# Attention scores as products of 64 rows, two maps in the two halves of the array

## The chip, the cores and the metric

The kernel runs on one core of a Trainium2 chip. A core has a matrix engine (TensorE, "PE" in the profile, with its weight loads listed apart as "PEld"), a vector engine (VectorE, "DVE"), a scalar engine (ScalarE, "ACT"), GpSimd ("POOL") and a sync engine ("SP") that issues most transfers. The metric is the device time of one execution in microseconds; the figure is the median of the runs.

## The reference

The program is a two-layer encoder over 1024 tokens of width 1024, all in float32. Each layer is a token mixer, a layer norm, a gated feed-forward net and another layer norm. Layer 0 mixes by latent attention, layer 1 by *differential* attention, and only that second mixer is touched here:

```python
q, k, v = split(x @ w_in)          # q, k: 8 heads x 2 maps x 64; v: 8 heads x 128
logits = einsum('bqhmd,bkhmd->bmhqk', q_b, k) * scale      # m = 2 maps, d = 64
logits = logits - slopes[:, None, None] * dist
logits = where(chunk_mask, logits, -1e30)
p = softmax(logits, axis=-1)
a = p[:, 0] - lam * p[:, 1]
o = einsum('bhqk,bkhe->bqhe', a, v)
```

So each head has two score maps. Each map contracts over only 64 numbers, which is half of the 128 rows of the matrix array. The mask lets a block of 128 queries see the keys up to its own block, so block i (0 to 7) has n = 128 (i+1) keys.

## The kernel before, in words

Precision is held by splitting every float32 operand into a high part (rounded to fp32r, a format that the array takes in one pass) and a low part (the rest). A product is then the sum of three: high by high, high by low, low by high. The helper `mm3` (lines 139 to 145) writes these three out for ordinary products: projections of queries and keys ("bp" tiles, 24 matmuls of 128x512 each), values ("bv" tiles, 24 of 128x256).

The second attention is built by `attention` (one loop over 64 blocks: 8 heads by 8 query blocks). For each block it makes the scores two blocks ahead (`score_b`), transposes the finished probabilities of this block (`turn_b`), every second block multiplies by the values (`mix_b`), and in between it runs the projections of the next head and the values of the next pair of heads out of a table of slots (`fill`). The calls give the program order. A list scheduler then interleaves the instructions of each engine by priority; scores and transposes carry a higher priority (`tc.high_priority`) than the projections, so that TensorE gets projections where the others are not ready. Each engine runs its own stream in that fixed order.

The scores need the two maps of 64 rows kept apart. Before, `proj_b` laid the data out so that *two* products of the full 128 rows make one map's scores:

- keys: one tile per map, with the high part in one half of the rows and the low part in the other half (lines 1413 and 1414, per map);
- queries, high: the high part in one half of the rows (line 1403), copied by a DMA from the POOL queue to the other half (line 1407), so that one product gives high by high plus high by low;
- queries, low: the low part in the half that faces the keys' high part (line 1404) and zeros in the other half. The zeros are written once (lines 1360 to 1366).

`softmax_block` (line 206) then does one map at a time. For each stretch of at most 512 keys (one for n up to 512, two equal ones above) it takes a bank of the accumulator memory PSUM, runs the two matmuls of line 220 (stationary: 128 queries; moving: the keys), and lets VectorE add the distance bias and take the row minimum (line 223). ScalarE takes the exponential over all n keys (line 228). Then `score_b` normalizes, GpSimd scales the second map (line 1430) and VectorE adds both (line 1431).

PSUM has eight banks in this stage. `PS_BUFS_B = (3, 2, 2, 1)` gives three to the scores (and to the sums of the head norm, "ms"), two to projections and values, two to transposes, and one to the value products. A tile of a kind takes the banks of its kind in turn.

Of the kernel before, what the change touches and what calls it, by code (L numbers as in the profile page):

```python
# [9 lines left out]
F32 = mybir.dt.float32  # L10
F32R = mybir.dt.float32r
AF = mybir.ActivationFunctionType
ALU = mybir.AluOpType
# [3 lines left out]
P = 128  # L17
S = 1024
# [16 lines left out]
BIGF = 3.0e38  # L35
PS_BUFS = (4, 2, 2)
PS_BUFS_A = (2, 3, 3)
PS_BUFS_B = (3, 2, 2, 1)
LAST_ORDER = (6, 7, 4, 5, 2, 3, 0, 1)


# [1 line left out]
def trunk(  # L43
# [32 lines left out]
    nc = tc.nc  # L76
    V, A, G, T = nc.vector, nc.scalar, nc.gpsimd, nc.tensor
# [11 lines left out]
    ps, ps_bufs, ps_stack = None, None, None  # L89
# [17 lines left out]
    def f32(t):  # L107
        return t.bitcast(F32)

    def big_tile(name, dt=F32R):  # L110
        return big.tile([P, 2, 1024], dt, tag="big", name=name)

    def ps_s(name):
        return ps.tile([P, 512], F32, tag="s", bufs=ps_bufs[0], name=name)
# [2 lines left out]
        return ps.tile([P, 512], F32, tag="m", bufs=ps_bufs[1], name=name)  # L117

    def ps_t(name):
        return ps.tile([P, 512], F32, tag="t", bufs=ps_bufs[2], name=name)  # L120

    def ps_o(name):
# [2 lines left out]
    def small(name, n=1):  # L125
        return sp.tile([P, 2], F32, tag="small", name=name, bufs=22)[:, :n]
# [28 lines left out]
    def behind(i, j):  # L155

        tc.add_manual_dep(
            i, j.name,
            mybir.DependencyInfo(mybir.DependencyClass.NoSync, mybir.DependencyReason.DATA),
            reason="kept in program order",  # L160
        )
# [48 lines left out]
    def softmax_block(lp, q_pass, s_bias, i, scale, name, sm=None):  # L210
        n = (i + 1) * P
        nb = 1 if n <= 512 else 2
        w = n // nb
        l = lp.tile([P, 1024], F32, tag="l", name=f"l_{name}")
        mx = BIGF
        for b in range(nb):
            s = ps_s(f"s_{name}_{b}")
            ks = slice(b * w, (b + 1) * w)
            for j, (lh, rh) in enumerate(q_pass):
                T.matmul(s[:, :w], lh, rh[:, ks], start=(j == 0), stop=(j == len(q_pass) - 1))  # L220
            bv = s_bias[:, 896 - P * i + b * w:896 - P * i + (b + 1) * w]
            m = small(f"mx_{name}_{b}")
            V.tensor_tensor_reduce(l[:, ks], s[:, :w], bv, -scale, mx, ALU.add, ALU.min, m)  # L223
            mx = m
        whole = sm is None
        if whole:
            sm = small(f"sm_{name}")
        ends["exp"] = A.activation(l[:, :n], l[:, :n], AF.Exp, bias=mx, scale=-1.0, accum_out=sm).ins  # L228
        if not whole:
            return l  # L230
        r = small(f"r_{name}")
        V.reciprocal(r, sm)
        return l, r
# [830 lines left out]
    with tc.tile_pool(name="a0", bufs=2, side="right") as pool:  # L1064
# [42 lines left out]
        with tc.issue_after(third):  # L1107
            kt = pool.tile([P, NTB, P], F32, tag="kt", name="kt", bufs=1)
# [83 lines left out]
    with ast as st:  # L1192
        pool = st.enter_context(tc.tile_pool(name="a1", bufs=2, reuse_waits="tile"))
        vp = st.enter_context(tc.tile_pool(name="a1v", bufs=12, side="right", reuse_waits="tile"))
        lp = st.enter_context(tc.tile_pool(name="a1l", bufs=4, side="right", reuse_waits="tile"))
# [105 lines left out]
        for h in range(1, H):  # L1301
            b = 8 * (h - 1)
# [32 lines left out]
    def split_wo(h, c):  # L1335
# [6 lines left out]
    xT, rest, normed = ffn(  # L1342
        "left", xo, stacks, pending, 0, xs_dr[0], xs_dr[1], ln_ffn_g[0], ln_ffn_b[0], next_x,
        [lambda h=h, c=c: split_wo(h, c) for h in range(H) for c in range(2)],
    )
# [3 lines left out]
    with ExitStack() as st:  # L1349
        lp = st.enter_context(tc.tile_pool(name="b1l", bufs=5, reuse_waits="tile"))  # L1350
# [2 lines left out]
        bb = pool.tile([P, S], F32, tag="bb", name="bb", bufs=1)  # L1353
        nc.sync.dma_start(bb, c_bias_b)
        vt, lt, pts, sqs, q_slot = {}, {}, {}, {}, {}
        qt = [big_tile(f"bq{j}") for j in range(2)]
        kt = [big_tile(f"bk{j}") for j in range(2)]
        ob = big_tile("bo", F32)
        q_hi = [qt[0][:, 0], qt[0][:, 1], qt[1][:, 0]]
        q_lo = [qt[1][:, 1]] + [pool.tile([P, S], F32R, tag=f"ql{j}", name=f"ql{j}", bufs=1) for j in range(2)]  # L1360
        for ql in q_lo:
            for mp in range(2):
                b = slice(64 - mp * 64, 128 - mp * 64)
                z = bb[b, :512]
                i = G.tensor_tensor(ql[b, mp * 512:mp * 512 + 512], z, z, ALU.subtract).ins
                behind(i, normed[-1][2])

        def values_b(pr, tb):
            if ("v", pr) not in wts:
# [17 lines left out]
        def proj_b(h, which, hf):  # L1387
            if (which, h) not in wts:
                wts[which, h] = load_w(w_b_qk[h, which], 1024, f"wb{h}_{which}")
            wh, wl = wts[which, h]  # L1390
            hs = slice(hf * 512, hf * 512 + 512)
            m = ps_m(f"bp{h}_{which}_{hf}")
            mm3(m, [(wh[:, k * P:k * P + P], wl[:, k * P:k * P + P], xT[0][hf][:, k, :], xT[1][hf][:, k, :])
                    for k in range(KD)])
            sc = float(2.0 ** (h + 1) / 8.0)
            if which == 0:
                j = 2 * h + (hf if h < H - 1 else 1 - hf)
                q2, ql = q_slot[h, hf] = q_hi[j % 3], q_lo[j % 3]
                for mp in range(2):
                    a = slice(mp * 64, mp * 64 + 64)  # L1400
                    b = slice(64 - mp * 64, 128 - mp * 64)
                    qh = q2[:, mp * 512:mp * 512 + 512]
                    A.activation(qh[a], m[a, :], AF.Copy, scale=sc)
                    V.scalar_tensor_tensor(
                        ql[a, mp * 512:mp * 512 + 512], m[a, :], sc, f32(qh[a]), ALU.mult, ALU.subtract
                    )
                    nc.gpsimd.dma_start(qh[b], qh[a])
            else:
                for mp in range(2):
                    a = slice(mp * 64, mp * 64 + 64)  # L1410
                    b = slice(64 - mp * 64, 128 - mp * 64)
                    k = kt[h % 2][:, mp]
                    A.copy(k[a, hs], m[a, :])
                    V.tensor_tensor(k[b, hs], m[a, :], f32(k[a, hs]), ALU.subtract)

        def score_b(h, i):
            c = slice((i % 4) * P, (i % 4) * P + P)
            n = (i + 1) * P
            (q2, ql), k = q_slot[h, i // 4], kt[h % 2]
            sm, r = small(f"smb{h}_{i}", 2), small(f"rb{h}_{i}", 2)  # L1420
            l0, l1 = [
                softmax_block(
                    lp,
                    [(t[:, m * 512:m * 512 + 512][:, c], k[:, m]) for t in (q2, ql)],
                    bb, i, float(2.0 ** -(h + 1)), f"b{h}_{i}_{m}", sm[:, m:m + 1],
                )
                for m in range(2)
            ]
            V.reciprocal(r, sm)  # L1429
            G.tensor_scalar(l1[:, :n], l1[:, :n], r[:, 1:2], nlam, ALU.mult, ALU.mult)  # L1430
            V.scalar_tensor_tensor(l0[:, :n], l0[:, :n], r[:, 0:1], l1[:, :n], ALU.mult, ALU.add)
            lt[h, i] = l0
# [67 lines left out]
        for h in range(1, H):  # L1500
            b = 8 * (h - 1)
# [124 lines left out]
```

## Time and profile before

| | |
|---|---|
| median of 3 runs | 2262.74 us (2262.04 to 2263.79) |
| the profiled execution's own time | 2264.72 us |
| its span, first to last instruction | 2263.0 us |
| TensorE busy | 2239.2 us (99%), 11410 instructions |
| VectorE, ScalarE, GpSimd busy | 1545.3, 1014.7, 776.2 us |
| mean granted TensorE clock | 0.998 |
| first and last score product of the second attention start at | 1125.8 and 1532.1 us |

The profile lists, for each engine, when each instruction ran, how long, and what the engine waited for. A matmul's record runs from its start until its result is out, so records of neighbouring matmuls overlap; how much time one takes from the stream is read from start to start. "64x512" after a name is partitions by elements. Lines are those of the kernel before.

### The profile page before, as it was taken

Reading aid. Unit: us, or ns where it says so; the run is one execution under the profiler, and the core shown is the slowest. Engines: PE = TensorE matmul, PEld = TensorE weight load, DVE = VectorE, ACT = ScalarE, POOL = GpSimd, SP = SyncE. Lnnn points to the kernel's source line nnn. Section 1 sums busy time; section 2 is a strip of 40 time slices with the busy share of each in tenths; the row PEclk is TensorE's granted clock in tenths of the full one; section 3 lists DMA queues with packets and bytes.
Section 4 is the critical chain, followed back from the end, with each engine's and each line's share of the span. In section 5 each row is a group of like instructions: output and inputs, shape, how many; then the busy total and the mean of one; then the engine's idle time right before and its main releaser. Section 6 shows DMA issues by size and latency. Waiting matters only on the chain.

```text
span 2263.0 us, 31059 instructions
## 1 busy us (share of the span) xinstructions
PE 2239.2 (99%) x11410; PEld 1912.2 (84%) x11410; DVE 1545.3 (68%) x2894; ACT 1014.7 (45%) x2097; POOL 776.2 (34%) x626
## 2 busy tenths in 40 slices
PE   8999999999999999999999999999999999999998
PEld 8999998888888888888888898878788888888886
DVE  5676765596766667777576667576787656658778
ACT  4455664352333334444465656564432333334444
POOL 2232341114444440455432424221114444430561
PEclk9999999999999999999999999999999999999999
DMA  5010125434435338454320212063344232238443
GB/s 204 14 35 31 42 71 188 147 122 155 171 133 202 115 127 327 181 194 157 99 52 22 69 34 62 23 223 124 128 144 165 82 108 102 103 113 325 162 180 150
DMA packets 105545, 287.76 MB, mean 127 GB/s; under 512 B 7968, under 2 KB 30112, under 8 KB 94896
## 3 DMA queue, kind: packets, MB, share of 16 engines
q1 hardware_dynamic: 101552, 277.44, 34.6%
q0 software_dynamic: 3840, 8.33, 1.4%
q8 instruction: 90, 1.47, 0.3%
q14 instruction: 63, 0.52, 0.1%
HBM read 204.47 MB, written 77.07 MB: 124 GB/s over the span
## 4 chain that ended last, share of the span: by engine, by line
PE 95%; DVE 2%; DMA 1%; issue 1%; ACT 1%; POOL 0%; SPq 0%; DVEq 0%; POOLq 0%; ACTq 0%
PE gb L548 15%; PE ga L548 10%; PE gc L548 10%; PE dw L872 7%; PE dx L872 5%; PE s_a L220 4%; PE zp_a L418 3%; PE s_b L220 3%; PE dv L872 3%; PE dy L872 3%; PE bp L145 3%; PE bp L143 3%; PE bp L144 3%; PE o_a L263 2%; PE o_b L263 2%; PE hq L1123 2%
## 5 line engine op out<-in xcount | busy, mean ns | idle before, releaser
L504 ACT CAST op_g<-gr 128x512 fp32r<-128x512 f32 x240 | 146.9, 621 | 377.3 <-PE gb L548 189.9
L505 POOL TENSOR_TENSOR op_g<-gr,op_g 128x512 fp32r<-128x512 f32 x104 | 146.0, 1409 | 254.1 <-ACT op_g L504 143.9
L505 DVE TENSOR_TENSOR op_h<-rh,op_h 128x512 fp32r<-128x512 f32 x152 | 142.3, 962 | 50.0 <-ACT op_h L504 50.0
L548 PE MATMUL ga<-xh_m,op_g 128*128 128x512 f32 x512 | 168.2, 389 | 0.0
L872 PE MATMUL dw<-op_w_t,op_h 128*128 128x512 f32 x660 | 151.3, 390 | 0.0
L504 ACT CAST op_h<-rh 128x512 fp32r<-128x512 f32 x152 | 91.8, 619 | 124.6 <-PE dx L872 34.9
L872 PEld LDWEIGHTS dw<-op_w_t,op_h 128*128 128x128 f32 x660 | 123.6, 188 | 25.9 <-DVE op_h L505 0.3
L228 ACT ACTIVATE l_b<-l_b,mx_b 128x256 f32<-128x256 f32 (+7 forms) x128 | 99.4, 777 | 73.2 <-DVE mx_b L223 71.2
L505 POOL TENSOR_TENSOR op_w_b<-rw_b,op_w_b 128x512 fp32r<-128x512 f32 x44 | 64.5, 1488 | 175.1 <-ACT op_w_b L504 167.8
L505 DVE TENSOR_TENSOR op_g<-gr,op_g 128x512 fp32r<-128x512 f32 x136 | 112.0, 827 | 17.4 <-ACT op_g L504 17.2
L872 PE MATMUL dx<-op_w_b,op_h 128*128 128x512 f32 x528 | 121.5, 390 | 1.0 <-DVE op_w_b L505 1.0
L1430 POOL TENSOR_SCALAR l_b<-l_b,rb,cst 128x128 f32<-128x128 f32 (+3 forms) x64 | 52.8, 825 | 198.9 <-DVE rb L1429 187.5
L872 PEld LDWEIGHTS dx<-op_w_b,op_h 128*128 128x128 f32 x528 | 98.8, 188 | 23.0 <-DVE op_w_b L505 2.6
L548 PE MATMUL gb<-t3h_f,op_g 128*128 128x512 f32 x352 | 115.5, 389 | 1.0 <-DVE tmp L637 1.0
L548 PE MATMUL gb<-t2h_f,op_g 128*128 128x512 f32 x352 | 115.4, 390 | 0.4 <-DVE op_g L505 0.4
L548 PE MATMUL gc<-t1h_f,op_g 128*128 128x512 f32 x352 | 115.6, 389 | 0.1
L548 PE MATMUL gb<-t4h_f,op_g 128*128 128x512 f32 x352 | 115.5, 389 | 0.0
L548 PE MATMUL gc<-b22h_f,op_g 128*128 128x512 f32 x352 | 115.3, 389 | 0.0
L505 POOL TENSOR_TENSOR op_g<-s,op_g 128x512 fp32r<-128x512 f32 x40 | 56.1, 1403 | 166.4 <-ACT op_g L504 158.4
L548 PEld LDWEIGHTS ga<-xh_m,op_g 128*128 128x128 f32 x512 | 96.1, 188 | 20.0
L143 PE MATMUL bp<-xT_f,h_wb 128*128 128x512 f32 x256 | 101.8, 398 | 0.0
L144 PE MATMUL bp<-xT_f,h_wb 128*128 128x512 f32 x256 | 101.5, 397 | 0.0
(388 smaller groups left out, 6690.8 us busy)
## 6 DMA issues: line engine op xcount, KB each, us to landing
gr<-in_w_gu SPq DMA_DIRECT2D x44, 1024.0 KB, 6.8
rh<-h_dr SPq DMA_DIRECT2D x28, 1024.0 KB, 4.8
h_dr<-sh SPq DMA_DIRECT2D x22, 1024.0 KB, 5.1
h_dr<-hp SPq DMA_DIRECT2D x22, 768.0 KB, 4.1
tt<-in_w_dn SPq DMA_DIRECT2D x22, 512.0 KB, 7.5
rh<-h_dr SPq DMA_DIRECT2D x12, 768.0 KB, 4.3
wo_dr<-op_pwo SPq DMA_DIRECT2D x16, 512.0 KB, 3.4
z<-xs_dr SPq DMA_DIRECT2D x16, 512.0 KB, 12.0
```

Source lines behind the costliest of these rows:

```text
L143: T.matmul(ps_out, lh, rh, start=(i == 0), stop=False)
L144: T.matmul(ps_out, lh, rl, start=False, stop=False)
L145: T.matmul(ps_out, ll, rh, start=False, stop=(i == n - 1))
L220: T.matmul(s[:, :w], lh, rh[:, ks], start=(j == 0), stop=(j == len(q_pass) - 1))
L228: ends["exp"] = A.activation(l[:, :n], l[:, :n], AF.Exp, bias=mx, scale=-1.0, accum_out=sm).ins
L263: T.matmul(po[:, c], a, b[:, j % 2, c], start=st, stop=sp_, skip_group_check=True)
L418: T.matmul(m, a[:, h, :], self.wo[h][w][:, c], start=(start and h == heads[0] and a is oh and w == 0), stop=(stop and h == heads[-1] and a ...
L504: turns["cast"] = A.copy(hi, src).ins
L505: return eng.tensor_tensor(lo, src, f32(hi), ALU.subtract).ins
L548: T.matmul(o, w[:, a, k * P:(k + 1) * P], x[b][:, k, :], start=(first and k == 0 and (a, b) == (0, 0)), stop=(k == 3 and a == 1), skip_gro ...
L872: T.matmul(o, h[:, a, c], w[:, b_], start=(first and (a, b_) == (0, 0)), stop=(last and a == 1), skip_group_check=True,).ins for a, b_ in ...
L1430: G.tensor_scalar(l1[:, :n], l1[:, :n], r[:, 1:2], nlam, ALU.mult, ALU.mult)
```

## The change

Only the scores of the second attention are written in another way. Queries and keys now keep the rows that the projection gives them: map 0 in rows 0 to 63, map 1 in rows 64 to 127, a tile for the high parts and a tile for the low parts, of queries (`q_rot`, three slots in turn) and of keys (`kt`). Their extraction from PSUM is one instruction over 128 rows on ScalarE and one on VectorE where there were two each over 64 rows. The copy by DMA and the zeroed halves go.

`score_b` no longer calls `softmax_block`. For each stretch of keys it takes two banks, one per map, and runs three pairs of matmuls: high by high, high by low, low by high, each for map 0 (rows 0 to 63) and then for map 1 (rows 64 to 127). `behind` ties each of these six matmuls after the one before it, which fixes their order among themselves; it does not keep other matmuls from standing between. The bias, minimum, exponential and all that follows are the same instructions on the same shapes.

The banks are dealt as `(5, 2, 0, 1)`: scores, norm sums and transposes take five banks in turn.

```diff
@@ -35,7 +35,7 @@
 BIGF = 3.0e38
 PS_BUFS = (4, 2, 2)
 PS_BUFS_A = (2, 3, 3)
-PS_BUFS_B = (3, 2, 2, 1)
+PS_BUFS_B = (5, 2, 0, 1)
 LAST_ORDER = (6, 7, 4, 5, 2, 3, 0, 1)
 
 
@@ -117,6 +117,8 @@
         return ps.tile([P, 512], F32, tag="m", bufs=ps_bufs[1], name=name)
 
     def ps_t(name):
+        if not ps_bufs[2]:
+            return ps_s(name)
         return ps.tile([P, 512], F32, tag="t", bufs=ps_bufs[2], name=name)
 
     def ps_o(name):
@@ -1353,17 +1355,11 @@
         bb = pool.tile([P, S], F32, tag="bb", name="bb", bufs=1)
         nc.sync.dma_start(bb, c_bias_b)
         vt, lt, pts, sqs, q_slot = {}, {}, {}, {}, {}
-        qt = [big_tile(f"bq{j}") for j in range(2)]
+        qt = big_tile("bq").rearrange("p a (b t) -> p (a b) t", b=2)
         kt = [big_tile(f"bk{j}") for j in range(2)]
         ob = big_tile("bo", F32)
-        q_hi = [qt[0][:, 0], qt[0][:, 1], qt[1][:, 0]]
-        q_lo = [qt[1][:, 1]] + [pool.tile([P, S], F32R, tag=f"ql{j}", name=f"ql{j}", bufs=1) for j in range(2)]
-        for ql in q_lo:
-            for mp in range(2):
-                b = slice(64 - mp * 64, 128 - mp * 64)
-                z = bb[b, :512]
-                i = G.tensor_tensor(ql[b, mp * 512:mp * 512 + 512], z, z, ALU.subtract).ins
-                behind(i, normed[-1][2])
+        q_more = pool.tile([P, 2, 512], F32R, tag="bq", name="bq2", bufs=1)
+        q_rot = [(t[:, j], t[:, j + 1]) for t, j in ((qt, 0), (qt, 2), (q_more, 0))]
 
         def values_b(pr, tb):
             if ("v", pr) not in wts:
@@ -1395,37 +1391,42 @@
             sc = float(2.0 ** (h + 1) / 8.0)
             if which == 0:
                 j = 2 * h + (hf if h < H - 1 else 1 - hf)
-                q2, ql = q_slot[h, hf] = q_hi[j % 3], q_lo[j % 3]
-                for mp in range(2):
-                    a = slice(mp * 64, mp * 64 + 64)
-                    b = slice(64 - mp * 64, 128 - mp * 64)
-                    qh = q2[:, mp * 512:mp * 512 + 512]
-                    A.activation(qh[a], m[a, :], AF.Copy, scale=sc)
-                    V.scalar_tensor_tensor(
-                        ql[a, mp * 512:mp * 512 + 512], m[a, :], sc, f32(qh[a]), ALU.mult, ALU.subtract
-                    )
-                    nc.gpsimd.dma_start(qh[b], qh[a])
+                qh, ql = q_slot[h, hf] = q_rot[j % 3]
+                A.activation(qh, m, AF.Copy, scale=sc)
+                V.scalar_tensor_tensor(ql, m, sc, f32(qh), ALU.mult, ALU.subtract)
             else:
-                for mp in range(2):
-                    a = slice(mp * 64, mp * 64 + 64)
-                    b = slice(64 - mp * 64, 128 - mp * 64)
-                    k = kt[h % 2][:, mp]
-                    A.copy(k[a, hs], m[a, :])
-                    V.tensor_tensor(k[b, hs], m[a, :], f32(k[a, hs]), ALU.subtract)
+                kh, kl = (kt[h % 2][:, p, hs] for p in range(2))
+                A.copy(kh, m)
+                V.tensor_tensor(kl, m, f32(kh), ALU.subtract)
 
         def score_b(h, i):
             c = slice((i % 4) * P, (i % 4) * P + P)
             n = (i + 1) * P
-            (q2, ql), k = q_slot[h, i // 4], kt[h % 2]
+            nb = 1 if n <= 512 else 2
+            w = n // nb
+            (qh, ql), (kh, kl) = q_slot[h, i // 4], (kt[h % 2][:, p] for p in range(2))
             sm, r = small(f"smb{h}_{i}", 2), small(f"rb{h}_{i}", 2)
-            l0, l1 = [
-                softmax_block(
-                    lp,
-                    [(t[:, m * 512:m * 512 + 512][:, c], k[:, m]) for t in (q2, ql)],
-                    bb, i, float(2.0 ** -(h + 1)), f"b{h}_{i}_{m}", sm[:, m:m + 1],
-                )
-                for m in range(2)
-            ]
+            l0, l1 = ls = [lp.tile([P, 1024], F32, tag="l", name=f"l_b{h}_{i}_{m}") for m in range(2)]
+            mx = [BIGF, BIGF]
+            for b in range(nb):
+                ks = slice(b * w, (b + 1) * w)
+                s = [ps_s(f"s_b{h}_{i}_{m}_{b}") for m in range(2)]
+                prev = None
+                for j, (q, k) in enumerate(((qh, kh), (qh, kl), (ql, kh))):
+                    for m in range(2):
+                        rows = slice(64 * m, 64 * m + 64)
+                        t = T.matmul(s[m][:, :w], q[rows, c], k[rows, ks], start=(j == 0), stop=(j == 2)).ins
+                        if prev is not None:
+                            behind(t, prev)
+                        prev = t
+                bv = bb[:, 896 - P * i + b * w:896 - P * i + (b + 1) * w]
+                for m in range(2):
+                    mx[m], mp = small(f"mx_b{h}_{i}_{m}_{b}"), mx[m]
+                    V.tensor_tensor_reduce(
+                        ls[m][:, ks], s[m][:, :w], bv, -float(2.0 ** -(h + 1)), mp, ALU.add, ALU.min, mx[m]
+                    )
+            for m in range(2):
+                A.activation(ls[m][:, :n], ls[m][:, :n], AF.Exp, bias=mx[m], scale=-1.0, accum_out=sm[:, m:m + 1])
             V.reciprocal(r, sm)
             G.tensor_scalar(l1[:, :n], l1[:, :n], r[:, 1:2], nlam, ALU.mult, ALU.mult)
             V.scalar_tensor_tensor(l0[:, :n], l0[:, :n], r[:, 0:1], l1[:, :n], ALU.mult, ALU.add)
```

Line numbers behind the changed places move by one or two. The three pieces below are of TensorE's stream. `s_b_5_0_0` is the score tile of block 5; before, the last two numbers are map and stretch, and so they are now. `bp` is a query or key projection, `ms` a norm sum, `pt_b` a transpose.

In the fifth head, block 5, the stream before has:

```order
L1461 MATMUL ms_0_1_13311<-sq_0_13191,ones 128x512
L143 MATMUL bp_0_1_13361<-xT_f_10052,h_wb_0_13274 128x512
L220 MATMUL s_b_5_0_0_13326<-bk_10191,bq_10189 128x384
L144 MATMUL bp_0_1_13361<-xT_f_10053,h_wb_0_13274 128x512
L220 MATMUL s_b_5_0_0_13326<-bk_10191,bq_10190 128x384
L145 MATMUL bp_0_1_13361<-xT_f_10052,l_wb_0_13275 128x512
L143 MATMUL bp_0_1_13361<-xT_f_10052,h_wb_0_13274 128x512
```

and the changed kernel at the same place:

```order
L1462 MATMUL ms_0_1_13347<-sq_0_13227,ones 128x512
L145 MATMUL bp_0_1_13401<-xT_f_10052,h_wb_0_13314 128x512
L1418 MATMUL s_b_5_0_0_13363<-bk_10190,bq 128x384
L146 MATMUL bp_0_1_13401<-xT_f_10053,h_wb_0_13314 128x512
L1418 MATMUL s_b_5_1_0_13364<-bk_10190,bq 128x384
L147 MATMUL bp_0_1_13401<-xT_f_10052,l_wb_0_13315 128x512
L1418 MATMUL s_b_5_0_0_13363<-bk_10190,bq 128x384
L145 MATMUL bp_0_1_13401<-xT_f_10052,h_wb_0_13314 128x512
L1418 MATMUL s_b_5_1_0_13364<-bk_10190,bq 128x384
L146 MATMUL bp_0_1_13401<-xT_f_10053,h_wb_0_13314 128x512
L1418 MATMUL s_b_5_0_0_13363<-bk_10190,bq 128x384
L147 MATMUL bp_0_1_13401<-xT_f_10052,l_wb_0_13315 128x512
```

The two score products of map 0 became three for each map, and here a projection over all 128 rows stands between each two of them. In the first head, block 5, the changed stream has the form that recurs most where the six are not wholly apart:

```order
L1418 MATMUL s_b_5_0_0_10788<-bk_10190,bq 128x384
L145 MATMUL bp_1_0_10972<-xT_f_10050,h_wb_1_10968 128x512
L146 MATMUL bp_1_0_10972<-xT_f_10051,h_wb_1_10968 128x512
L1418 MATMUL s_b_5_1_0_10789<-bk_10190,bq 128x384
L1418 MATMUL s_b_5_0_0_10788<-bk_10190,bq 128x384
L1418 MATMUL s_b_5_1_0_10789<-bk_10190,bq 128x384
L1418 MATMUL s_b_5_0_0_10788<-bk_10190,bq 128x384
L1418 MATMUL s_b_5_1_0_10789<-bk_10190,bq 128x384
L1418 MATMUL s_b_5_0_1_10800<-bk_10190,bq 128x384
```

The first product of map 0 stands alone, five follow in one run, and the next stretch begins right behind them. Over the whole stage the 384 score products of before are 576 now. They stand in 252 unbroken runs: 158 of one product, 22 of two, 15 of three, 13 of four, 22 of five, 11 of six, 5 of seven, and 6 longer ones with 66 products together. Ahead of the second attention TensorE's stream is the same in both kernels, and so is that of most of the last feed-forward net.

## The prediction

> **What bounds the kernel now.** I read the page's head, the busy shares and the chain of waits first:
>
> ```profile
> span 2263.0 us, 31059 instructions
> ...
> PE 2239.2 (99%) x11410; PEld 1912.2 (84%) x11410; DVE 1545.3 (68%) x2894; ACT 1014.7 (45%) x2097; POOL 776.2 (34%) x626
> ...
> PE 95%; DVE 2%; DMA 1%; issue 1%; ACT 1%; POOL 0%; SPq 0%; DVEq 0%; POOLq 0%; ACTq 0%
> ```
>
> TensorE carries the chain over the whole program. So does it in the stage of the change, from the first score product to the end of the attention. Here are the busy times of the five engines in that stretch (the columns are the stretch, its length, then PE, PEld, DVE, ACT, POOL, clock, DMA), and below it the same for the score tiles alone (PE, PEld, DVE):
>
> ```profile
> 1125.00:1540.00 415.00, 412.31 (x2508) 364.96 (x2507) 284.49 (x795) 247.16 (x572) 135.21 (x128) 1.00 0.23 72
> ```
> ```profile
> 1125.00:1540.00 415.00, 100.75 (x384) 64.15 (x384) 109.19 (x192) 1.00 0.23 72
> ```
>
> TensorE has nothing in flight for 2.7 of 415 us, VectorE is at 69% and ScalarE at 60%. What this change is worth is therefore what it does to TensorE's stream. The 100.75 us of the 384 score products is not that: records overlap. What a product takes is the distance from its start to the next start, and the timeline of TensorE shows it:
>
> ```profile
> 1300.39 0.34 PE L220 MATMUL s_b<-bk,bq 128*128 128x384 f32 x1
> 1300.57 0.34 PE L220 MATMUL s_b<-bk,ql 128*128 128x384 f32 x1
> 1300.74 0.28 PE L143 MATMUL bv<-h_wbv,xT_f 128*128 128x256 f32 x1
> 1300.86 0.28 PE L144 MATMUL bv<-l_wbv,xT_f 128*128 128x256 f32 x1
> ...
> 1304.70 0.36 PE L220 MATMUL s_b<-bk,bq 128*128 128x448 f32 x1
> 1304.90 0.37 PE L220 MATMUL s_b<-bk,ql 128*128 128x448 f32 x1
> ...
> 1305.51 0.39 PE L143 MATMUL bp<-xT_f,h_wb 128*128 128x512 f32 x1
> 1305.74 0.39 PE L144 MATMUL bp<-xT_f,h_wb 128*128 128x512 f32 x1
> 1305.97 0.40 PE L145 MATMUL bp<-xT_f,l_wb 128*128 128x512 f32 x1
> ...
> 1310.93 0.39 PE L144 MATMUL bp<-xT_f,h_wb 128*128 128x512 f32 x1
> 1311.17 0.82 PE L148 MATMUL pt_b<-ident,l_b 128*128 128x128 f32 x6
> 1311.74 0.48 PE L220 MATMUL s_b<-bk,bq 128*128 128x512 f32 x1
> 1312.06 0.39 PE L220 MATMUL s_b<-bk,ql 128*128 128x512 f32 x1
> 1312.29 0.39 PE L220 MATMUL s_b<-bk,bq 128*128 128x512 f32 x1
> ```
>
> From start to start: 0.227 us for 512 columns (two steps in 0.46), 0.20 for 448, 0.175 for 384, 0.12 for 256, so by a straight line 0.147 for 320. From 1311.17 to 1312.06, 0.89 us, pass six transposes of 128 columns and one product of 512; less its 0.227 that is 0.11 for each transpose, where the columns alone would ask for half of the 256 case. A floor is at work there. The weight loads show which:
>
> ```profile
> 1490.08 0.19 PEld L263 LDWEIGHTS o_b<-pth_b,bvh 128*128 128x128 f32 x1
> 1490.20 0.19 PEld L263 LDWEIGHTS o_b<-ptl_b,bvh 128*128 128x128 f32 x1
> ...
> 1492.00 0.19 PEld L263 LDWEIGHTS o_b<-ptl_b,bvh 128*128 128x128 f32 x1
> 1492.11 0.19 PEld L263 LDWEIGHTS o_b<-pth_b,bvl 128*128 128x128 f32 x1
> ```
>
> Each product brings a load of 128 columns; at 256 columns loads stand 0.12 apart and hide, at 128 columns they stand 0.11 apart and set the pace. I take 0.11 us as the least distance of two loads.
>
> **The change part by part.** *Products removed.* Per head, two products per map and stretch: 64 stretches-and-maps over 512 columns wide work out, over all heads, to 96 products of 512, 64 of 448, 96 of 384, 64 of 320, 32 of 256, 32 of 128 (together the 384 of the row above). 96x0.227 + 64x0.20 + 96x0.175 + 64x0.147 + 32x0.12 + 32x0.11 = 68.2 us of stream.
>
> *Products added.* Half as many again: 576, each over 64 rows. If two of them in different halves run side by side and all six of a stretch stood together, three steps would take the place of four: 51.1 us. But the order of the changed stream, shown above, breaks the sixes up. A projection, a transpose or a value product uses all rows, so beside it no half is free. Going through the 252 runs with the same steps, a run of products that alternate between the halves costing what its busier half costs: the 158 lone products take 28.1 us, the 22 twos 3.7, the threes 5.0, the fours 4.6, the fives 11.0, the sixes 6.9, the sevens 3.7, the longer ones 6.1. That is 69.0 us: **+0.9 us against before, where the loads hide.** Loads cannot hide if they come one at a time, 0.11 apart: a pair of 320 columns needs two loads, 0.22, for 0.147 of stream. With that floor within each run the same sum is 28.1 + 6.1 + 5.8 + 6.6 + 13.4 + 8.4 + 4.2 + 7.8 = 80.5 us (80.4 in the rounded terms): **+12.3.** If halves never overlap, each product costs its whole step, 102.2 us: **+34.1.** The trace has no product over 64 rows, so 0.9 and 34.1 are the bounds; I take 12.3, because nothing in the rows lets two loads come closer than 0.11, while side-by-side streaming of two halves asks only that each half be free.
>
> The Trainium skill speaks to the load. In "TensorE: Matmul & The Clock Gate", section "LDWEIGHTS (loading the stationary operand)", a load's time goes by its columns and not its rows, with a rule that gives some 107 ns for 128 columns; the trace's 0.11 agrees for full rows, and by this a load of 64 rows would be no cheaper.
>
> *Changes of shape.* Each run is entered from products over 128 rows and left to them: 2x252 = 504 changes that before did not have. No row shows one. Below, the nearest row is the change between products and transposes: the product ahead of the six transposes takes 0.24 (1310.93 to 1311.17) against 0.227, and the 0.89 with them holds nothing over; so 0 to some 10 ns a change, at most 5 us in all. Above, a change could wait until the array is empty: a 512-column record lasts 0.39 and its step is 0.227, so 0.16 each, 82 us in all; or it could only stop the next load from being made ahead, as at the first product behind the transposes, whose own step is 0.32 (1311.74 to 1312.06), 0.09 over 0.227; 504 of them would be 45 us. I take 10 ns, **+5.0 us**, by the row that is a change of kind within the stream, and keep 0 and 82.
>
> *Evictions.* Here are the queries' rows; the keys' rows (lines 1413 and 1414) follow the same pattern:
>
> ```profile
> L1403 ACT ACTIVATE bq<-bp x32: 576/593/596, 1096.3 to 1470.2; 64x512 fp32r<-64x512 f32 x32
> L1407 POOL DMA_DIRECT2D bq<-bq x32: 528/564/575, 1099.9 to 1472.4; - x32
> L1404 DVE SCALAR_TENSOR_TENSOR ql<-bp,bq x20: 671/688/695, 1097.0 to 1458.7; 64x512 fp32r<-64x512 f32 x20
> ```
>
> An instruction over 128 partitions and 512 elements takes the place of two over 64 and 512. As its length per partition is the same, I give it the same time: ScalarE loses 16 of 32 for queries and as many for keys, 32 x 0.593 = 19 us; VectorE 32 x 0.688 = 22 us; the POOL queue 32 issues of 0.564 and GpSimd six zeroing instructions. All of it lies beside TensorE, which idles 2.7 us in the stage, so its worth is 0. Were that cover gone, the most would be the 22 us of VectorE, in the gain's direction.
>
> *Banks.* Five banks in turn serve scores and transposes instead of three and two. A block above 512 keys takes four score banks and then two transposes' banks, one more than there are; the sixth waits until VectorE has read the first. VectorE reads a 512-column score tile in:
>
> ```profile
> L223 DVE CUSTOM_DVE_ANT_0 l_b<-s_b,bb 128x512 f32<-128x512 f32 x32 | 21.8, 683 | 2.2 <-PE s_b L220 2.0
> L223 DVE CUSTOM_DVE_ANT_0 l_b<-s_b,bb,mx_b 128x512 f32<-128x512 f32 x16 | 11.9, 746 | 0.6
> ```
>
> Behind a waiting score product on TensorE stand the projections, which nothing else holds. Before, TensorE's waits in the stage were these, columns being the total, the times and the longest:
>
> ```profile
> PE s_b L220 <- DVE mx_b L223: 1.0, 3, 0.6
> PE pt_b L148 <- DVE l_b L1431: 0.8, 2, 0.6
> PE zp_a L418 <- DMA wo<-wo_dr: 0.7, 1, 0.7
> ```
>
> With three banks and one map at a time this was 1.0 us. I give the new banks 0 (one tile is read two tiles before it is due again) and keep -1 to +22 (32 blocks of over 512 keys, one wait of 0.68 each).
>
> **Sum.** 12.3 + 5.0 + 0 + 0 = +17.3 us on the profiled execution's own 2264.7 us is 2282.0. That execution lies 2.0 us above the median of the runs shown, so the forecast is 2280 us.
>
> **The rivals.**
>
> *Loads hide too* (no change). Then 69.0 us for 68.2 and changes of shape free: 2262.7 + 0.9, 2264 us. For it: loads already run during other products in every row above. Against it: the 0.11 that the loads keep even where the columns would let them come closer. The Trainium skill's "TensorEngine Tiling (Array Packing)", section "Key Properties", says that different tiles can load and multiply in parallel; that is this case, and no run here shows it yet.
>
> *A change of shape empties the array* (slower by more). 504 x 0.09 = 45 us with only the load lost, 82 us with the full tail, on 69.0 or 80.5: from 2262.7 + 0.9 + 45 = 2309 upward to 2262.7 + 12.3 + 82 = 2357. For it: the broken order makes it dear, twice per run. Against it: transposes come and go for nothing. The same section of "TensorEngine Tiling (Array Packing)" states that changing the tiling mode, not just the tile, drains the TensorE; it gives no time for it.
>
> *The halves never overlap* (slower): 2262.7 + 34.1 = 2297 us, if the array takes one product at a time whatever its rows. The change then does not do what its name says. Nothing in this trace speaks for or against it.
>
> *The waits near the end go* (faster). Place: the last head, where no projections are left to fill. These two rows there start after the engine idled, in the brackets:
>
> ```profile
> 1493.96 0.47 PE L220 MATMUL s_b<-bk,bq 128*128 128x448 f32 x1 [0.25 <-DVE mx_b L223]
> 1495.23 0.50 PE L220 MATMUL s_b<-bk,bq 128*128 128x512 f32 x1 [0.59 <-DVE mx_b L223]
> ```
>
> The scores wait there for VectorE to free one of three banks. Five banks and a stage freed of 22 us of VectorE's work could take these away: the 2.7 us of idle time, and about as much again that hides under the records' tails. It decides only if loads hide and shapes change for nothing: 2262.7 + 0.9 - 2 x 2.7 = 2258 us.
>
> *Banks bind* (slower): the 22 us above on 69.0, 2285 us. Against it: the scheduled order puts projections between nearly all sixes, so VectorE gets its time.
>
> **How the numbers follow.** Chances: the forecast 0.38 (its own range 2268 to 2295), loads hide 0.17, the array is emptied 0.18, no overlap 0.12, end waits go 0.10, banks bind 0.05. A change below 0.2%, 4.5 us, is about what a measurement of this kernel can't tell from none: within 2258.2 to 2267.3. Slower takes the forecast, the emptied array, no overlap and banks, 0.73 less 0.02 for the forecast's lower edge: 0.71. Same takes 0.13 of the hidden loads and 0.03 from the edges of its neighbours: 0.16. Faster is the remaining 0.13. The range is 2256 to 2318: it keeps nearly all of the first, second and fourth case, half of the fifth and the lower part of the emptied array, and leaves out 0.16.
>
> **What would show it.** In the changed profile the score products have 64 rows and number 576. Two of one run starting within 30 ns of each other show overlap; a steady 0.11 between starts in a run shows the load's floor; starts a full step apart show none. A change of shape shows in the first step of a lone score product between two projections: 0.18 for 384 columns if it is free, 0.27 and more if the load or the array is lost. The stage from the first score product on should last about 432 us instead of 415, with TensorE's listed waits still under 5 us. If they are above 15, the banks bind. The forecast is wrong if the stage stays within 4 us of 415, or if lone products cost over 50 ns more than their columns.

## The result, and the profile after

The changed kernel takes 2393.57 us (median of 6 runs, 2375.95 to 2400.33) against 2263.55 us for the kernel before on the same chip. The ratio is 1.056, with a 95% interval of 1.055 to 1.058: 130 us slower, where +17 was forecast and 2318 us was the upper end of the range.

The page of the changed kernel, its span, busy shares, chain and granted clock (in tenths, over 40 equal slices):

```profile
span 2398.6 us, 31251 instructions
...
PE 2371.7 (99%) x11602; PEld 1943.6 (81%) x11602; DVE 1525.3 (64%) x2862; ACT 993.2 (41%) x2064; POOL 745.0 (31%) x588
...
PEclk9999999999999999999998978989999999999999
...
PE 94%; DVE 2%; ACT 1%; issue 1%; POOL 1%; DMA 1%; SPq 0%; POOLq 0%; DVEq 0%; ACTq 0%
```

TensorE is as busy as before, 99%, and still carries the chain. The new thing is the clock, which falls below full in the stage of the change. Below is that stage in stretches (length, then PE, PEld, DVE, ACT, POOL busy, then clock, DMA share and GB/s), the score tiles alone (PE, PEld, DVE), and TensorE's waits in the stage (total, times, longest):

```profile
1124.00:1240.00 116.00, 116.00 (x632) 85.98 (x631) 66.06 (x201) 55.41 (x136) 29.93 (x27) 0.99 0.12 37
1240.00:1280.00 40.00, 40.00 (x166) 28.05 (x166) 12.05 (x36) 11.46 (x28) 4.82 (x5) 0.79 0.04 14
1280.00:1400.00 120.00, 119.74 (x640) 89.16 (x639) 61.71 (x171) 52.20 (x125) 29.24 (x23) 0.96 0.10 32
1400.00:1480.00 80.00, 80.00 (x267) 52.86 (x267) 25.66 (x70) 22.44 (x48) 14.23 (x10) 0.72 0.08 27
...
sum 547.00, PE 545.03 PEld 396.35 DVE 267.79 ACT 227.06 POOL 115.56; mean PE 77.86 PEld 56.62 DVE 38.26 ACT 32.44 POOL 16.51
```
```profile
1124.00:1671.00 547.00, 146.09 (x576) 69.71 (x576) 105.81 (x192) 0.92 0.14 47
```
```profile
PE s_b L1418 <- DVE ptl_b L254: 1.1, 1, 1.1
PE pt_b L150 <- DVE ptl_b L254: 0.5, 2, 0.3
PE s_b L1418 <- DVE mx_b L1425: 0.3, 1, 0.3
```

The stage lasts 547 us where 415 was before; the rest of the program lasts 1851.6 us where it lasted 1848.0. TensorE has something in flight for 545 of the 547 us and waits for others for 1.9 us in all. So no bank and no other engine holds it up: its own stream became longer. The timeline shows where. First a run of six products of 512 columns, then a lone product of 320:

```profile
1132.66 0.39 PE L145 MATMUL bp<-xT_f,h_wb 128*128 128x512 f32 x1
1132.89 0.27 PE L150 MATMUL pt_b<-ident,l_b 128*128 128x128 f32 x1
1133.09 0.98 PE L1418 MATMUL s_b<-bk,bq 64*128 64x512 f32 x6
1134.00 0.50 PE L146 MATMUL bp<-xT_f,h_wb 128*128 128x512 f32 x1
1134.34 0.39 PE L147 MATMUL bp<-xT_f,l_wb 128*128 128x512 f32 x1
1134.57 0.39 PE L145 MATMUL bp<-xT_f,h_wb 128*128 128x512 f32 x1
...
1135.27 0.38 PE L150 MATMUL pt_b<-ident,l_b 128*128 128x128 f32 x2
1135.58 0.41 PE L1418 MATMUL s_b<-bk,bq 64*128 64x320 f32 x1
1135.92 0.50 PE L145 MATMUL bp<-xT_f,h_wb 128*128 128x512 f32 x1
1136.26 0.40 PE L146 MATMUL bp<-xT_f,h_wb 128*128 128x512 f32 x1
```

**The halves do run side by side.** Six products of 512 columns pass in 0.91 us (1133.09 to 1134.00). One after the other they would need 6 x 0.227 = 1.36; three steps of pairs are 0.68.

**Each change of shape costs about 0.20 us.** Read the lone product. The two transposes ahead of it take 0.31 (1135.27 to 1135.58), where 2 x 0.11 is their due: 0.09 more. The product itself takes 0.34 where 320 columns are 0.147: 0.19 more. The projection behind it takes 0.34 (1135.92 to 1136.26) where 0.227 is due: 0.11 more. Together that is 0.39 us beside the product's own 0.147. The six show the same: 0.09 ahead, 0.91 - 0.68 = 0.23 inside, 0.11 behind, 0.43 in all. Over the visits in the trace that fall wholly into the full clock, the medians are 0.10 ahead, 0.20 inside and 0.10 behind.

What these pieces are is seen in the weight loads of the same place:

```profile
1132.66 0.14 PEld L150 LDWEIGHTS pt_b<-ident,l_b 128*128 128x128 f32 x1
1133.09 0.54 PEld L1418 LDWEIGHTS s_b<-bk,bq 64*128 64x128 f32 x6 [0.29 <-issue]
1134.00 0.19 PEld L146 LDWEIGHTS bp<-xT_f,h_wb 128*128 128x128 f32 x1 [0.37 <-issue]
1134.11 0.19 PEld L147 LDWEIGHTS bp<-xT_f,l_wb 128*128 128x128 f32 x1
```

The load of the first score product starts at 1133.09, with the product itself and not during the one before. So does the load of the projection that follows, at 1134.00. Among products of one shape a load runs ahead, as 1134.11 is for the product of 1134.34. So at each change the next load begins 0.09 late and is then exposed (0.11). I read the 0.09 as the array emptying; the profile shows the late load and not the array, and the ends of records are modelled. Twice 0.20 makes about 0.40 for each visit to 64 rows, that is, for each run of such products between products over 128. The six loads also take 0.54 us from first to last end, where loads 0.11 apart would need 5 x 0.11 + 0.19 = 0.74: loads of the two halves go in parallel. In the trace's records the first two loads start 3 ns apart, and so do their products.

**The clock.** Where the stream changes shape with every product, the clock falls. The same view around 1402 us, while the clock is still full, and around 1404 us, where it is at half:

```profile
1401.52 0.41 PE L1418 MATMUL s_b<-bk,bq 64*128 64x320 f32 x1
1401.86 0.39 PE L146 MATMUL bv<-l_wbv,xT_f 128*128 128x256 f32 x1
1402.17 0.41 PE L1418 MATMUL s_b<-bk,bq 64*128 64x320 f32 x1
...
1403.48 0.62 PE L1418 MATMUL s_b<-bk,bq 64*128 64x320 f32 x1
1404.03 0.58 PE L146 MATMUL bv<-l_wbv,xT_f 128*128 128x256 f32 x1
1404.54 0.63 PE L1418 MATMUL s_b<-bk,bq 64*128 64x320 f32 x1
1405.10 0.58 PE L147 MATMUL bv<-h_wbv,xT_f 128*128 128x256 f32 x1
```

A score product and a value product take 0.65 us together at full clock (1401.52 to 1402.17): 0.147 + 0.12 for their columns, and 0.38 for the visit. At half clock the same two take 1.06 (1403.48 to 1404.54). Here the alternation comes first and the fall of the clock behind it. TensorE's records leave no gap there: from 1445 to 1461 us, for one, it is busy for 16.00 of 16 us at a mean clock of 0.50.

How much of the 130 us is the clock can be read from the six timed executions: their mean granted clocks run from 0.980 (2400.33 us) to 0.992 (2375.95), and all six lie within 1.2 us of a straight line of 20.5 us for each 0.01. At 0.998, the clock of the kernel before, that line gives 2364 us. This is an estimate, as none of the six ran above 0.992. By it some 100 us are the stream at full clock, and the remaining 30 of the median are the lost clock. The sum for the first is 0.9 us for the products, as worked out before, and 252 x 0.40 = 101.

### The profile page after: what moved, and what is told of

Read it like the earlier page. It is cut to its first block, busy times and chain, and to the rows that moved or that the text cites. A ratio compares the mean times of both kernels' runs of the same rounds, so it can differ in the third digit from the quotient of the medians.

```text
span 2398.6 us, 31251 instructions
## 1 busy us (share of the span) xinstructions
PE 2371.7 (99%) x11602; PEld 1943.6 (81%) x11602; DVE 1525.3 (64%) x2862; ACT 993.2 (41%) x2064; POOL 745.0 (31%) x588
## 4 chain that ended last, share of the span: by engine, by line
PE 94%; DVE 2%; ACT 1%; issue 1%; POOL 1%; DMA 1%; SPq 0%; POOLq 0%; DVEq 0%; ACTq 0%
PE gb L550 14%; PE ga L550 10%; PE gc L550 10%; PE dw L874 7%; PE dx L874 5%; PE s_b L1418 5%; PE s_a L222 3%; PE zp_a L420 3%; PE bp L145 3%; PE bp L147 3%; PE bp L146 3%; PE dv L874 2%; PE dy L874 2%; PE o_a L265 2%; PE o_b L265 2%; PE pt_b L150 2%
## 5 line engine op out<-in xcount | busy, mean ns | idle before, releaser
L1418 PE MATMUL s_b<-bk,bq 64*128 64x512 f32 (+5 forms) x576 | 146.1, 418 | 1.4 <-DVE ptl_b L254 1.1
L874 PEld LDWEIGHTS dw<-op_w_t,op_h 128*128 128x128 f32 x660 | 123.7, 188 | 25.6
L253 ACT CAST pth_b<-pt_b 128x256 fp32r<-128x256 f32 (+1 forms) x160 | 54.0, 347 | 191.0 <-PE pt_b L150 171.3
L1418 PEld LDWEIGHTS s_b<-bk,bq 64*128 64x128 f32 x576 | 69.7, 192 | 57.6 <-issue 34.7
```

The source lines that it names most:

```text
L874: T.matmul(o, h[:, a, c], w[:, b_], start=(first and (a, b_) == (0, 0)), stop=(last and a == 1), skip_group_check=True,).ins for a, b_ in ...
L1418: t = T.matmul(s[m][:, :w], q[rows, c], k[rows, ks], start=(j == 0), stop=(j == 2)).ins
```

## The experiments

The theory (called A in the expectations): what costs the time is the change between products over 128 rows and products over 64, about 0.40 us a visit, and nothing else in the change does. Its rival (B): the broken order, the larger number of products or the shared banks. All ratios below are to the kernel before on the same chip, measured beside each run.

### The same products over all rows

```diff
-                        rows = slice(64 * m, 64 * m + 64)
-                        t = T.matmul(s[m][:, :w], q[rows, c], k[rows, ks], start=(j == 0), stop=(j == 2)).ins
+                        t = T.matmul(s[m][:, :w], q[:, m * 512:m * 512 + 512][:, c], k[:, ks], start=(j == 0), stop=(j == 2)).ins
```

This is the line that matters. The query tiles are twice as wide, with zeros in the other map's half, as the low parts had them before the change, and are filled by instructions over 64 rows again.

> The same 576 score products in the same pairs, with the same five banks, but each over all 128 rows: the queries of each map carry zeros in the other map's half, so no product uses a part of the array. The sixes are as broken up as in the change (246 runs). Theory A (what costs is the change between products over 128 rows and products over 64): no such change is left, each product costs its full step, 102.2 us for 68.2 before, so 2263.5 + 34 = about 2298 us, with the clock at 1.00 all through the stage. Theory B (the broken order, the number of products or the shared banks cost the time): about as slow as the change, 2380 to 2400 us.

Measured: 2303.41 us, ratio 1.018 (1.016 to 1.019), +39 us where A said +34 and B at least +117. TensorE's stage in this kernel, with the clock full:

```profile
1125.00:1575.00 450.00, 447.04 (x2691) 397.32 (x2690) 284.66 (x774) 234.27 (x552) 117.13 (x98) 1.00 0.16 57
```

576 products, five banks and an order as broken as in the change (246 runs) cost 39 us. B falls: products over 64 rows, half the work for the array, are 90 us dearer than the same products over 128 rows filled up with zeros.

### Added products, over 64 rows and over 128

```diff
             ks = slice(b * w, (b + 1) * w)
+            if not whole:
+                d = slice(0, 64)
+                T.matmul(s[:, :P], q_pass[0][0][d], q_pass[0][1][d, :P], start=True, stop=True)
             for j, (lh, rh) in enumerate(q_pass):
```

This is the kernel before, with `whole = sm is None` moved ahead so that only the second attention has it; the second kernel has `slice(0, 128)`.

> The kernel before, with one added product of 64 rows and 128 columns ahead of the real products of each of the 192 score tiles (its result is overwritten by the first real product, so nothing else changes). Each stands between products over 128 rows. Theory A (each visit to 64 rows costs 0.20 on the way in and 0.20 on the way out, beside its own columns of 0.055): 192 x 0.40 to 0.46, +77 to +88, so 2341 to 2352 us. A theory in which only scattered pairs or the five banks cost time would give what a 128-row product of that size costs: 192 x 0.11 at most, 2285 us.

> The same added product over all 128 rows: 192 x 0.055 to 0.11 by any theory, +11 to +21, so 2274 to 2285 us. The difference to the run with 64 rows is the price of 192 visits, free of banks, pairs and order.

Measured: 2346.61 us over 64 rows, ratio 1.036 (1.035 to 1.038), and 2288.18 us over 128, 1.010 (1.009 to 1.012). The first is +82.5 us, 0.43 for each of 192; the second +24.0, 0.125 each, a little above the 0.11 that I gave as the most. The difference, 58.4 us or 0.30 us each, is what 64 rows cost more than 128 for the same small product, in a kernel with neither pairs nor shared banks. One such visit in the timeline, between a projection and the real products of its tile:

```profile
1302.18 0.39 PE L145 MATMUL bp<-xT_f,l_wb 128*128 128x512 f32 x1
1302.41 0.39 PE L143 MATMUL bp<-xT_f,h_wb 128*128 128x512 f32 x1
1302.72 0.32 PE L222 MATMUL s_b<-bk,bq 64*128 64x128 f32 x1
1302.98 0.33 PE L224 MATMUL s_b<-bk,bq 128*128 128x128 f32 x1
```

The projection ahead of it takes 0.31 instead of 0.227, so 0.08 more, and the added product 0.26, so 0.20 more than its columns. Of the 0.43 us of a visit that leaves 0.09 behind it. Those are the three pieces of the change, shown here by themselves.

### Fewer visits

```diff
-        attention(score_b, turn_b, mix_b, fill, 2, (0, 60))
+        attention(score_b, turn_b, mix_b, fill, 2, (400, 60))
```

The higher priority keeps most sixes from being broken again after their first product: 153 runs instead of 252. The control gives the same priority to the kernel before.

> The change with a higher priority for the scores, so that the 576 products stand in 153 runs instead of 252 (most of them one product and then five). Theory A, at 0.40 us for each visit to 64 rows (0.09 + 0.11 on the way in, the same on the way out): stream 62.4 + 153 x 0.40 = 123.6 us for 68.2 before, +55, so about 2319 us, and the clock hardly falls below 1.00. Theory B (banks or number of products): little changes, 2380 to 2400 us.

> The kernel before with the higher priority for the scores alone, a control for the kernels that use it. It moves no work on or off TensorE's stream: 2260 to 2268 us by theory A. If the priority itself made waits, it would be slower by more than 5 us, and the grouped kernels' numbers would have to be read against that.

Measured: 2317.85 us, ratio 1.024 (1.022 to 1.025), against 2319 by the sum. The control is 2267.58 us, 1.0015 (1.0005 to 1.0024), so the priority itself is worth about +3 us, which the sum doesn't hold. With 99 visits fewer, the kernel is 76 us faster than the change: some 40 for the visits, 7 for products that find their pair again (62.4 for 69.0), and about 30 for the clock. The clock is back, with 0.996 over the whole and this in the stage:

```profile
1124.00:1590.00 466.00, 461.91 (x2677) 355.97 (x2676) 265.21 (x762) 223.70 (x538) 117.00 (x99) 0.99 0.16 56
```

### The halves one after the other

```diff
-                for j, (q, k) in enumerate(((qh, kh), (qh, kl), (ql, kh))):
-                    for m in range(2):
+                for m in range(2):
+                    for j, (q, k) in enumerate(((qh, kh), (qh, kl), (ql, kh))):
```

This is made on the kernel with the higher priority.

> The change with higher priority, but the three products of one half ahead of the three of the other instead of in turn. 150 runs, most of them now three products of one half, so little runs side by side: a stream of 93.5 us instead of 62.4 at 153 runs. If two halves run side by side only where products of different halves stand next to each other, 2263.5 + 25.3 + 150 x 0.40 = 2349 us, 31 more than with the halves in turn. If the array finds the pairs by itself across the order, or if halves do not help at all, about 2318 us as with the halves in turn.

Measured: 2340.12 us, ratio 1.034 (1.033 to 1.036), 22 us more than with the halves in turn, where 31 were expected and 0 by the other reading. So the pairs are real. But they need not stand next to each other in the stream, as the few sixes show that stay whole in this order:

```profile
1133.85 0.27 PE L150 MATMUL pt_b<-ident,l_b 128*128 128x128 f32 x1
1134.05 0.98 PE L1418 MATMUL s_b<-bk,bq 64*128 64x512 f32 x6
1134.96 0.50 PE L145 MATMUL bp<-xT_f,h_wb 128*128 128x512 f32 x1
```

Six products, three of one half and then three of the other, pass in 0.91 us (1134.05 to 1134.96), as the six in turn did in the change; one after the other they would need 1.36. Their records start in twos, 10 ns apart. What counts is that products of both halves stand in one unbroken run. Here 108 of the 150 runs are three products of one half, and these find no partner. If each run costs what its busier half costs, the stream, worked out after the run, is 83.0 us instead of 93.5, and the sum 2263.5 + 14.8 + 150 x 0.40 = 2338 us, 2 below the measured time. That accounts for the 9 us by which the expectation was too high.

### The banks alone

```diff
-PS_BUFS_B = (3, 2, 2, 1)
+PS_BUFS_B = (5, 2, 0, 1)
...
     def ps_t(name):
+        if not ps_bufs[2]:
+            return ps_s(name)
         return ps.tile([P, 512], F32, tag="t", bufs=ps_bufs[2], name=name)
```

> The kernel before with the banks of the change alone: scores, norm sums and transposes share five in turn. Theory A: nothing on TensorE's stream moves, 2260 to 2268 us. The rival of my prediction that banks bind: 2285 us.

Measured: 2270.52 us, ratio 1.0032 (1.0019 to 1.0045), +7.7 us. That is more than nothing and a third of the 22 us of the rival. Most of it is waiting: by the pages TensorE is idle for 28.6 us of the span (2269.3 less 2240.7), where it was 23.8 before. From the stage on the listed waits are many small ones, none above 1.8 us, so no single place makes it up. The changed kernel, with the same banks, is idle for 26.9 us, 3 more than before, so little of its 130 us can be waiting for banks. They also fit the 39 us of the kernel over all rows, which has these banks and should by its products alone be +34.

### Whole sixes and whole blocks

To keep a six together for certain, its two banks become one tile, so that the first product cannot start before the second bank is free:

```diff
-PS_BUFS_B = (5, 2, 0, 1)
+PS_BUFS_B = (0, 2, 1, 1)
...
-                s = [ps_s(f"s_b{h}_{i}_{m}_{b}") for m in range(2)]
+                s2 = ps_group(f"s_b{h}_{i}_0_{b}")
+                s = [s2[:, m] for m in range(2)]
```

`ps_group` is a tile of two banks, of which there are two; norm sums and the transposes of the output projection take its two halves. In the second kernel it is one tile of four banks that holds all scores of a block, 6 or 12 products in one run. In the third, two-bank tiles again, transposes and value products share two banks in turn. All three have the higher priority.

> The change with the two banks of a stretch taken as one tile of two banks (two such tiles, one bank for transposes) and higher priority for the scores: the six products of a stretch now stand together, 84 runs in all. Theory A: stream 51.1 + 84 x 0.40 = 84.7 us for 68.2 before, +16.5, so about 2280 us; up to 8 us more if the single bank for transposes makes TensorE wait. If weight loads had a floor of 0.11 us in a run, as I had predicted, the stream would be 69.8 and the time 2299 us. Theory B: above 2340 us.

> As the kernel with sixes together, but all banks of a block are one tile of four banks and all its 6 or 12 products stand in one run: 64 runs. Theory A: 51.1 + 64 x 0.40 = 76.7 us for 68.2 before, +8.5, so about 2272 us, with some 0 to 8 us more for waits, since one tile of four banks must be read before the next block's scores. With a load floor of 0.11 us it would be 2291 us. Theory B: above 2340 us.

> Sixes together as in the kernel of two-bank tiles, but transposes and value products share two banks in turn instead of having one each, so that TensorE should wait less; 94 runs. Theory A: 51.1 + 94 x 0.40 = 88.7 us for 68.2 before: +20, so 2284 us without waits. If starved banks were what made the two grouped kernels slow, this should lie between 2284 and 2320; if it stays near 2365, something else of the grouping costs the time.

Measured: 2364.59 us (ratio 1.044, 1.043 to 1.046), 2367.88 us (1.046, 1.045 to 1.048) and 2315.78 us (1.023, 1.021 to 1.024). The first two miss their sums by 85 and 96 us, with only 84 and 64 visits. Their stages, first sixes, then whole blocks, then sixes with two shared banks:

```profile
1124.00:1620.00 496.00, 456.91 (x2681) 366.34 (x2681) 272.16 (x755) 222.95 (x534) 118.95 (x100) 0.93 0.15 53
```
```profile
1124.00:1620.00 496.00, 451.32 (x2693) 368.58 (x2691) 272.42 (x763) 225.87 (x541) 118.10 (x100) 0.93 0.15 53
```
```profile
1124.00:1565.00 441.00, 426.45 (x2652) 341.59 (x2650) 258.34 (x739) 216.24 (x520) 116.32 (x95) 0.99 0.16 57
```

TensorE now idles, 39 and 45 us of 496, and in the first kernel its longest waits, here over the whole program, are for VectorE to clear the banks of transposes and scores:

```profile
PE pt_b L161 <- DVE ptl_b L265: 13.8, 14, 2.2
PE s_b L1435 <- DVE mx_b L1442: 11.8, 12, 1.5
```

With that the clock falls to 0.93. At most 0.07 x 496 = 35 us are lost by it, an estimate, since a low clock costs nothing while TensorE idles. Idle time and clock together come near the misses: at most 74 of 85 and 80 of 96 us. The third kernel, in which transposes may use either of two banks, idles 15 us, has a clock of 0.99 and lies 32 us above its sum of 2284. So a good part of the miss is starved banks, as the third kernel shows; that the rest of it is the clock and a longer end, where the same tiles serve the output projection, is a reading of the profile and was not tried alone.

What these three show is the trade: whole sixes were had for banks, and in the first two kernels the banks cost more than whole sixes save (2364.59 and 2367.88 us, against 2317.85 for the broken sixes with the same priority). In the third the two are about even. By the sums alone even 64 visits (25.6 us) would be dearer than the 17 us that pairs save, so none of these kernels could beat the one before, and none did.

## Why the prediction was wrong

**What bounds the kernel.** Right: TensorE's stream bounds it before and after, and waits stayed at 1.9 us in the stage.

**Products removed and added.** Right, and shown by the runs: halves overlap only within a run, whose busier half sets its cost, the broken order undoes the gain, and the products come out even (69.0 for 68.2). The bound without overlap, +34.1, is nearly what the kernel over all rows measures, +39 with its banks.

**The load floor, +12.3.** Wrong. I took 0.11 us as the least distance of any two loads, from rows in which all loads fill the whole array. Loads of different halves go in parallel, so a pair of 320 columns does not need 0.22: in the changed profile six such products pass in 0.64 us (1138.64 to 1139.28), which is three steps of 0.147 and the 0.20 of a visit that falls inside. The Trainium skill's "TensorEngine Tiling (Array Packing)", section "Key Properties", states that different tiles load and multiply in parallel. The trace agrees, with loads of a pair 3 ns apart.

**Changes of shape, +5.0. This is the step that failed.** I counted the 504 changes, and kept 0 to 82 us for them, but took 10 ns by the row of the transposes. That row is a change of what is done with the data, not of how the rows are grouped, and it says nothing on the latter. The runs give 0.20 us each: 0.09 until the next load starts and 0.11 for that load, which cannot run ahead. These were my two upper candidates, 0.16 for the tail and 0.09 for the load, and I had set them up as one *or* the other. They come one behind the other. So even the bound was too low, 504 x 0.20 = 101 us. That the 0.09 for the load came near the measured 0.11 is luck: six transposes of 0.11 from 1311.17 on last until 1311.83, so the product behind them, with its record from 1311.74, only starts 0.09 early, and the seven together lose nothing. The same section of the Trainium skill states that a change of tiling mode drains the engine. The trace agrees, with a load that starts 0.09 us late at the changes shown, and the rival that I gave 0.18 was the case.

**The clock, not in the prediction.** Some 30 us of the 130. I had no term for it, since the clock was 0.998 over the kernel before. The 30 is read off the line through six executions and is an estimate.

**Evictions** at nothing: right as far as the profile shows, as ScalarE and VectorE had 21.5 and 20.0 us less work and TensorE waited 1.9 us in the stage. **Banks** at 0: measured +7.7 in the kernel before.

**The rivals.** "A change of shape empties the array" was the true one. Its range of 2309 to 2357 us ends 7 us below the 2364 that the change takes at full clock, and comes that near only with the 12.3 us of the load floor in it, which did not occur. "The halves never overlap" is not the case. "Loads hide too" is half of the truth: they hide within a run, never across a change. The range ended at 2318 because I gave weight to a row of another kind over the Trainium skill's statement on the drain, which has no figure.

## What to carry to other kernels

Before packing small products into halves of the array, count the visits: on this chip one visit from full-row products and back cost about 0.40 us, so a visit has to hold at least that much saved streaming, here more than three paired steps of 512 columns save over four full ones (0.23 us). Look at the order that the scheduler makes, not at the loop: products that stand together in the code stood in 252 runs in the stream. Count the runs and what each holds of both halves; the order within a run made no difference to the six shown. Where the rest of the stream is full-row, filling the other half with zeros or with a second term can be cheaper than packing.

## What was not expected of the hardware

- The granted clock falls to half in parts of a stage in which TensorE always has a product in flight (80.00 of 80 us busy at a mean clock of 0.72, and 16.00 of 16 at 0.50), where single products alternate in shape. It is 0.99 over the stage when the same products stand in 153 runs. Visits alone do not bring it down: with 192 lone added products it stayed at 0.999. What exactly the clock goes by is not shown here.
- Two loads for different halves start together, 3 ns apart in the trace's records; two loads for the whole array never came closer than about 0.11 us in the rows shown.
- Products of the two halves overlap within a run even when three of one half stand ahead of three of the other: six of 512 columns in 0.91 us in either order.
- A product over 64 rows between full-row products costs 0.30 us more than the same product over 128 rows.
